# Softmax minus one-hot on one core: six row buffers used as pair, row, pair, row

## The chip, the cores and the metric

The kernel runs on 1 core of one Trainium2 chip. The time is that of the device, in microseconds, from one launch of the program; the median of the runs is compared. The profile is one execution of the same program, taken by the hardware profiler.

## The reference

The kernel computes the gradient of a cross entropy with respect to the logits: softmax along the last axis, minus one at the label. There are 8 x 1024 = 8192 vectors of 8192 float32, so 268.4 MB come in and 268.4 MB go out.

```python
batch, seq_len, vocab = 8, 1024, 8192
logits_max = np.max(logits, axis=-1, keepdims=True)
exp_logits = np.exp(logits - logits_max)
softmax = exp_logits / np.sum(exp_logits, axis=-1, keepdims=True)
one_hot[batch_idx, seq_idx, labels] = 1.0
return (softmax - one_hot).astype(np.float32)
```

## The kernel before, in words

The 8192 vectors are cut into B = 32 blocks of 256. In a block, partition p owns the two vectors 2p and 2p+1, which are neighbours in memory: 64 KB in one run. A "row" in this document is one vector for each of the 128 partitions, that is, one half j = 0 or 1 of a block: a tile of 128 x 8192 float32, 4 MB, with 32 KB in each partition. There are T = 64 rows, t = 2 x block + j. A row is loaded by one DMA, in 128 runs of 32 KB whose starts lie 64 KB apart in memory, and it is stored in the same way from the same buffer.

The tile X holds R = 6 row buffers (three slots of G = 2). Row t uses buffer t mod 6. Five instructions work on a row, and everything is done in place in its buffer:

- DVE `row_max`: a reduction to the negative maximum.
- ACT `row_exp`: exp(x - max), with the sum beside it.
- DVE `invert`: the reciprocal of the sum, 128 numbers.
- ACT `row_scale`: the exponentials times that reciprocal.
- DVE `subtract`: minus one where the iota equals the label.

Three engines carry their own order, and semaphores tie them together. SP issues all 64 loads in the order of the rows; from row 6 on, a load waits until the store of the row that had the buffer before has landed (semaphore `put`, one for each buffer; `got` tells that a load has landed). DVE runs, for each row, `invert(k)`, `row_max(k+1)`, `subtract(k)`. ACT runs `row_scale(k)`, `row_exp(k+1)`, and then issues `store(k)`, which waits for `subtract(k)`. Loads therefore go through SP's DMA queue (q1 in the profile) and stores through ACT's (q10). Both queues are served by the same 16 DMA engines. Every load and every store is spread over all 16: each engine moves 8 runs and then writes 4 bytes, its part of the count on the semaphore.

DVE and ACT have loops over ten rounds of six rows, and four rows follow written out. The last row is scaled and subtracted in quarters and stored in two halves of 2 MB. At the end ACT waits for all stores.

Every instruction of the loops is recorded at the helper `run`, so in the profile they all stand under L67, and the tiles' names tell them apart: `m<-X` is `row_max`, `X<-X,m` is `row_exp`, `X<-X,r` is `row_scale`, `X<-iota,lab,X` is `subtract`, `X<-in_logits_dram` is a load and `out_dram<-X` a store.

Of the kernel before, what the change touches and what calls it, by code (L numbers as in the profile page):

```python
# [6 lines left out]

P = 128
G = 2
SLOTS = 3  # L10
R = SLOTS * G


LAST = 4


@with_exitstack
def kernel(
# [23 lines left out]
    psum = ctx.enter_context(tc.tile_pool(name="psum", bufs=1, space=bass.MemoryType.PSUM))  # L42


    X = const.tile([P, SLOTS, G, V], fp32)
    lab_raw = const.tile([B, G * P], labels.dtype)
    lab_f = const.tile([B, G, P], fp32)
    ident = const.tile([B, B], fp32)
    lab = const.tile([P, G, B], fp32)
# [5 lines left out]

    with tc.tile_critical():  # L56
        sem = tc.alloc_semaphore
        got = [[sem(f"got{i}{q}") for q in range(2)] for i in range(SLOTS)]
        put = [[sem(f"put{i}{q}") for q in range(2)] for i in range(SLOTS)]
        lab_got, dve, pe, pool = (sem(n) for n in ("lab_got", "dve", "pe", "pool"))  # L60
        count = {}

        def run(engine, waits, counter, method, **operands):

            for w in waits[:-1]:
                engine.wait_ge(*w)
            instruction = getattr(engine, method)(**operands)  # L67
# [15 lines left out]

        made = X[:, SLOTS - 1, G - 1, :].bitcast(i16)[:, :V]
# [23 lines left out]
        def slot(k):  # L108
            return X[:, k // G, k % G, :]

        def column(a, k):
            return a[:, k : k + 1]

        def load(t):
            b, j = divmod(t, G)
            k = t % R
            after = [(put[k // G][q], t // R * 16) for q in range(G)] if t >= R else []
            after = after[j : j + 1] or [w_iota] * (t == R - 1)
            run(nc.sync, after, got[k // G][j], "dma_start", out=slot(k), in_=x_b[b, :, j, :])

        def row_max(k, n):
            run(
                nc.vector, [(got[k // G][k % G], n)], max_of[k % G], "tensor_reduce",
                out=column(m, k), in_=slot(k), axis=mybir.AxisListType.X, op=Alu.max, negate=True,
            )

        def row_exp(k, n):
            run(
                nc.scalar, [(max_of[k % G], n)], exp_of[k % G], "activation", out=slot(k),
                in_=slot(k), func=Act.Exp, bias=column(m, k), scale=1.0, accum_out=column(s, k),  # L130
            )

        def invert(k, n):
            run(
                nc.vector, [(exp_of[k % G], n)], inv_of[k % G], "reciprocal",
                out=column(r, k), in_=column(s, k),
            )

        def row_scale(k, n, c=slice(0, V)):
            run(  # L140
                nc.scalar, [(inv_of[k % G], n)], scl_of[k % G], "activation", out=slot(k)[:, c],
                in_=slot(k)[:, c], func=Act.Copy, bias=0.0, scale=column(r, k),
            )

        def subtract(k, n, label, c=slice(0, V)):
            run(
                nc.vector, [(scl_of[k % G], n)], sub_of[k % G], "scalar_tensor_tensor",
                out=slot(k)[:, c], in0=iota[:, c], scalar=label, in1=slot(k)[:, c],
                op0=Alu.is_equal, op1=Alu.subtract, reverse1=True,
            )  # L150

        def store(k, n, target, c=slice(0, V)):
            run(
                nc.scalar, [(sub_of[k % G], n)], put[k // G][k % G], "dma_start",
                out=target[:, c], in_=slot(k)[:, c],
            )
# [6 lines left out]
        ROUNDS = T // R  # L163
        for t in range(T):
            load(t)

        row_max(0, 16)
        row_exp(0, 1)

        done = [counter(nc.vector, q + 1) for q in range(SLOTS)]  # L170
        landed = counter(nc.vector, 16)
        with nc.vector.Fori(0, ROUNDS * SLOTS, SLOTS) as b:  # L172
            for k in range(R):
                invert(k, done[k // G])
                if k == R - 1:
                    nc.vector.reg_add(landed, landed, 16)
                row_max((k + 1) % R, landed)
                subtract(k, done[k // G], lab[:, k % G, bass.ds(b + k // G, 1)])
            for reg in done:
                nc.vector.reg_add(reg, reg, SLOTS)  # L180

        done = [counter(nc.scalar, q + 1) for q in range(SLOTS)]
        with nc.scalar.Fori(0, ROUNDS * SLOTS, SLOTS) as b:
            for k in range(R):
                row_scale(k, done[k // G])
                if k == R - 1:
                    for reg in done[: SLOTS - 1]:
                        nc.scalar.reg_add(reg, reg, SLOTS)
                row_exp((k + 1) % R, done[(k + 1) % R // G])
                target = o_b[bass.ds(b + k // G, 1), :, k % G, :]  # L190
                store(k, done[k // G], target.rearrange("o p v -> (o p) v"))
            nc.scalar.reg_add(done[-1], done[-1], SLOTS)

        for t in range(ROUNDS * R, T - 1):
            k, n = t % R, t // G + 1
            invert(k, n)
            row_max(k + 1, 16 * (ROUNDS + 1))
            row_scale(k, n)
            row_exp(k + 1, n + k % G)
            subtract(k, n, lab[:, t % G, t // G : t // G + 1])  # L200
            store(k, n, o_b[t // G, :, t % G, :])
        k, n = (T - 1) % R, B
        invert(k, n)
        for q in range(4):
            c = slice(q * V // 4, (q + 1) * V // 4)
            row_scale(k, n, c)
            subtract(k, n + q, lab[:, G - 1, B - 1 : B], c)
        half = V // 2
        store(k, n + 1, o_b[B - 1, :, G - 1, :], slice(0, half))
        store(k, n + 3, o_b[B - 1, :, G - 1, :], slice(half, V))  # L210
        stored = {}
        for t in range(T):
            stored[t % R] = stored.get(t % R, 0) + 16
        stored[k] += 16
        for q in sorted(range(R), key=lambda q: (q - k - 1) % R):
            nc.scalar.wait_ge(put[q // G][q % G], stored[q])


# [28 lines left out]
```

## Time and profile before

| what | value |
|---|---|
| median of 3 runs | 1247.61 us (1247.56 to 1247.7) |
| the profiled execution's own time: its span, first to last instruction | 1245.6 us |
| DVE busy | 1121.8 us, 90% |
| ACT busy | 919.4 us, 74% |
| bytes moved by DMA | 536.95 MB, mean 431 GB/s |
| DMA packets on the load queue, on the store queue | 9216, 9408 |

No other time of the profiled execution is known than its span; the median of the runs is 2.0 us longer, and that difference is taken as what lies around the span. A share of DMA is the mean over the 16 engines of the time that their packets took; 1.00 means that all 16 always had a packet in work. A packet is counted where it starts, so in a window of few packets the shares and rates are coarse.

### The profile page before, as it was taken

To read this page: it belongs to the slowest core of one execution; us is meant where nothing else is said; L and a number is where in the kernel's file an instruction comes from. 1 tells how busy PE (TensorE), PEld (TensorE's weight loads), DVE (VectorE), ACT (ScalarE), POOL (GpSimd) and SP (SyncE) were. 2 spreads that over 40 slices of the span, in tenths; PEclk is the share of its full clock that TensorE was granted. 3 is DMA by queue.
4 is the path that set the end of the run, shared out by engine and by line. 5 is a ranking of instruction groups with operands and counts; after the bars stand their busy time and mean duration, and the time that the engine had idled before them with its cause. 6 is when DMAs were issued, how large, how long until landed. Compare 5 with 4: busy or idle time off the path is not lost.

```text
span 1245.6 us, 868 instructions
## 1 busy us (share of the span) xinstructions
PE 0.4 (0%) x2; PEld 0.3 (0%) x2; DVE 1121.8 (90%) x198; ACT 919.4 (74%) x196; POOL 7.4 (1%) x7
## 2 busy tenths in 40 slices
PE   0000000000000000000000000000000000000000
PEld 0000000000000000000000000000000000000000
DVE  5999999999988989889898898988988989889893
ACT  3888888888767777777767777677777777777772
POOL 2000000000000000000000000000000000000000
DMA  9999999999999999999999999999999999999999
GB/s 406 418 426 436 438 434 425 438 438 429 429 438 436 427 434 438 435 426 436 438 432 426 438 438 428 430 438 435 428 434 438 434 427 436 437 434 426 438 436 389
DMA packets 18625, 536.95 MB, mean 431 GB/s; under 512 B 2080, under 2 KB 2080, under 8 KB 2112
## 3 DMA queue, kind: packets, MB, share of 16 engines
q1 hardware_dynamic: 9216, 268.44, 50.0%
q10 hardware_dynamic: 9408, 268.51, 49.9%
q14 instruction: 1, 0.01, 0.0%
HBM read 268.50 MB, written 268.44 MB: 431 GB/s over the span
## 4 chain that ended last, share of the span: by engine, by line
another core or an unknown queue 67%; DVE 21%; DMA 6%; issue 2%; SPq 1%; DVEq 0%; ACT 0%; ACTq 0%; PE 0%
DVE m L67 11%; DVE X L67 10%; DMA out_dram<-X 4%; DMA X<-in_logits_dram 2%; SPq L67 1%; DVE iota L67 0%; DVE lab_f L67 0%; DMA lab_raw<-in_labels_dram 0%; DVEq L56 0%; ACT X L67 0%; DVE r L67 0%; PE iota L67 0%; ACTq L67 0%; DVEq L172 0%
## 5 line engine op out<-in xcount | busy, mean ns | idle before, releaser
L67 DVE TENSOR_REDUCE m<-X 128x1 f32<-128x8192 f32 x64 | 555.6, 8681 | 90.6 <-DMA X<-in_logits_dram 90.6
L67 ACT ACTIVATE X<-X,m 128x8192 f32<-128x8192 f32 x64 | 455.8, 7122 | 184.8 <-DVE m L67 184.8
L67 DVE SCALAR_TENSOR_TENSOR X<-iota,lab,X 128x8192 f32<-128x8192 int16 (+1 forms) x67 | 559.8, 8360 | 2.4 <-ACT X L67 2.4
L67 ACT ACTIVATE X<-X,r 128x8192 f32<-128x8192 f32 (+1 forms) x67 | 456.4, 6816 | 118.2 <-DVE r L67 118.2
L67 DVE RECIPROCAL r<-s 128x1 f32<-128x1 f32 x64 | 9.8, 153 | 7.3 <-ACT X L67 7.3
L67 ACT ACTIVATION_READ_ACCUMULATOR X<-X,m 128x1 f32 x64 | 11.9, 186 | 0.0
L67 DVE CAST lab_f<-lab_raw 32x256 f32<-32x256 int32 x1 | 3.8, 3784 | 4.6 <-DMA lab_raw<-in_labels_dram 4.6
L67 POOL IOTA X<- 128x8192 int16 x1 | 6.9, 6943 | 0.0
L67 DVE TENSOR_SCALAR iota<-X 128x4096 int32<-128x4096 int32 x1 | 4.4, 4428 | 0.1
L67 ACT ACT_TABLE_LOAD x1 | 1.3, 1283 | 1.4 <-SPq L56 1.4
L67 DVE COPY lab<-iota 128x64 f32<-128x64 f32 x1 | 0.2, 225 | 0.5 <-PE iota L67 0.5
L67 PE MATMUL iota<-ident,lab_f 32*128 32x32 f32 x2 | 0.4, 298 | 8.5 <-DVE lab_f L67 8.5
L67 PEld LDWEIGHTS iota<-ident,lab_f 32*128 32x128 f32 x2 | 0.3, 192 | 8.4 <-DVE lab_f L67 8.4
L67 POOL TENSOR_SCALAR_AFFINE_SELECT ident<-ident 32x32 f32<-32x32 f32 x1 | 0.2, 202 | 0.1
L67 POOL MEMSET ident<- 32x32 f32 x1 | 0.1, 114 | 0.5 <-SPq L56 0.5
L231 POOL MEMSET const-bfloat16-1.0<- 128x1 bf16 x1 | 0.1, 107 | 0.0
L231 POOL MEMSET const-uint8-127<- 128x1 uint8 x1 | 0.1, 107 | 0.0
L231 POOL MEMSET const-float32-0.0<- 128x1 f32 x1 | 0.1, 104 | 0.2 <-issue 0.2
L231 POOL MEMSET const-float32-1.0<- 128x1 f32 x1 | 0.1, 104 | 0.0
## 6 DMA issues: line engine op xcount, KB each, us to landing
X<-in_logits_dram SPq DMA_DIRECT2D x64, 4096.0 KB, 24.2
out_dram<-X ACTq DMA_DIRECT2D x63, 4096.0 KB, 55.2
out_dram<-X ACTq DMA_DIRECT2D x2, 2048.0 KB, 16.9
lab_raw<-in_labels_dram ACTq DMA_DIRECT2D x1, 64.0 KB, 3.7
```

The lines of the kernel that those rows point to most:

```text
L67: instruction = getattr(engine, method)(**operands)
L231: nc = _bacc.Bacc("TRN2", target_bir_lowering=False, num_devices=1)
```

## The change: what it does

The six buffers are seen as four units: a pair (buffers 0 and 1), a row (2), a pair (3 and 4), a row (5). In a cycle of six rows (three blocks, c = 0 to 9), the table `PLACES` gives each buffer its half-block: the first pair is both halves of the cycle's block 0, buffer 2 has half 0 of block 2, the second pair is block 1, and buffer 5 has half 1 of block 2. The third block is thus still moved in two separate rows, with another pair between them. After ten cycles four rows remain (`LAST_PLACES`).

A pair can be moved whole: one DMA of 8 MB with 128 runs of 64 KB. `whole_load` does so for 17 of the 20 pairs (all but the first three), `whole_store` for 18 of the 20 (all but the first and the last). So there are 47 load DMAs in place of 64, and 47 store DMAs (the two halves of the last row among them) in place of 65. The pairs at both ends and the last four rows are moved by row as before.

A whole store is issued once, after `subtract` of the pair's second row; a whole load waits for the store that empties both of its buffers, and `row_max` of a pair's second row needs no wait of its own. The instructions on DVE and ACT, their shapes and their order by row stay the same. Since the ends differ from the middle, the first two cycles on DVE and the first and the last on ACT are written out, and the loops cover the others.

```diff
+R = 6
+PLACES = ((0, 0), (0, 1), (2, 0), (1, 0), (1, 1), (2, 1))
+LAST_PLACES = ((0, 0), (0, 1), (1, 0), (1, 1))
+PAIRS = (0, 3)
...
+        def whole_load(c, k):
+            return c < CYCLES and k in PAIRS and c * len(PAIRS) + PAIRS.index(k) >= 3
+
+        def whole_store(c, k):
+            return k in PAIRS and 1 <= c * len(PAIRS) + PAIRS.index(k) < CYCLES * len(PAIRS) - 1
...
+        def pair(k):
+            return X[:, k : k + G, :].rearrange("p j v -> p (j v)")
...
+        def load(c, k, n):
+            after = [free_at[c - 1, i] for i in range(k, k + n)] if c else []
+            after = after[:1] if len(set(map(str, after))) == 1 else after
+            after = after or [w_iota] * (k == R - 1)
+            b, j = places(c)[k]
+            block = x_b[c * BLOCKS + b]
+            if n > 1:
+                run(
+                    nc.sync, after, got[k], "dma_start",
+                    out=pair(k), in_=block.rearrange("p j v -> p (j v)"),
+                )
+            else:
+                run(nc.sync, after, got[k], "dma_start", out=row(k), in_=block[:, j, :])
...
+        def store_pair(k, n, target):
+            run(
+                nc.scalar, [(sub_of[(k + G - 1) % G], n)], put[k], "dma_start",
+                out=target.rearrange("p j v -> p (j v)"), in_=pair(k),
+            )
...
+            for k in range(R):
+                b, j = PLACES[k]
                 row_scale(k, done[k // G])
...
                 row_exp((k + 1) % R, done[(k + 1) % R // G])
+                target = o_b[bass.ds(first + b, 1), :, :, :].rearrange("o p j v -> (o p) j v")
+                if k - 1 in PAIRS:
+                    store_pair(k - 1, done[k // G], target)
+                elif k not in PAIRS:
+                    store(k, done[k // G], target[:, j, :])
```

More of the change, by code (lines that the diff above doesn't have):

```diff
@@ L9 @@
 G = 2
-SLOTS = 3
-R = SLOTS * G
-LAST = 4
+R = 6
+PLACES = ((0, 0), (0, 1), (2, 0), (1, 0), (1, 1), (2, 1))
+LAST_PLACES = ((0, 0), (0, 1), (1, 0), (1, 1))
+PAIRS = (0, 3)
 @with_exitstack
@@ L57 @@
         sem = tc.alloc_semaphore
-        got = [[sem(f"got{i}{q}") for q in range(2)] for i in range(SLOTS)]
-        put = [[sem(f"put{i}{q}") for q in range(2)] for i in range(SLOTS)]
+        got = [sem(f"got{k}") for k in range(R)]
+        put = [sem(f"put{k}") for k in range(R)]
         lab_got, dve, pe, pool = (sem(n) for n in ("lab_got", "dve", "pe", "pool"))
@@ L111, in column, with row @@
+        def row(k):
+            return X[:, k, :]
+        def pair(k):
+            return X[:, k : k + G, :].rearrange("p j v -> p (j v)")
         def column(a, k):
             return a[:, k : k + 1]
[L114 to L119, printed above, removed]
@@ L121, in row_max @@
-        def row_max(k, n):
-            run(
-                nc.vector, [(got[k // G][k % G], n)], max_of[k % G], "tensor_reduce",
-                out=column(m, k), in_=slot(k), axis=mybir.AxisListType.X, op=Alu.max, negate=True,
+        units = [
+            (c, k, G if k in PAIRS and k + 1 < len(places(c)) else 1)
+            for c in range(CYCLES + 1)
+            for k in range(len(places(c)))
+            if k - 1 not in PAIRS
+        ]
+        landed, stored = [0] * R, [0] * R
+        loaded_by, free_at = {}, {}
@@ new lines @@
+        for c, k, n in units:
+            for q in [k] if whole_load(c, k) else range(k, k + n):
+                landed[q] += 16
+                for i in range(k, k + n) if whole_load(c, k) else [q]:
+                    loaded_by[c, i] = (got[q], landed[q])
+            for q in [k] if whole_store(c, k) else range(k, k + n):
+                stored[q] += 16 + 16 * ((c, k) == units[-1][:2] and q == k + n - 1)
+                for i in range(k, k + n) if whole_store(c, k) else [q]:
+                    free_at[c, i] = (put[q], stored[q])
@@ L125, in row_max @@
+        for c, k, n in units:
+            if whole_load(c, k):
+                load(c, k, n)
+            else:
+                for q in range(k, k + n):
+                    load(c, q, 1)
+        def row_max(k, waits):
+            run(
+                nc.vector, waits, max_of[k % G], "tensor_reduce",
+                out=column(m, k), in_=row(k), axis=mybir.AxisListType.X, op=Alu.max, negate=True,
             )
@@ L147, in subtract @@
                 nc.vector, [(scl_of[k % G], n)], sub_of[k % G], "scalar_tensor_tensor",
-                out=slot(k)[:, c], in0=iota[:, c], scalar=label, in1=slot(k)[:, c],
+                out=row(k)[:, c], in0=iota[:, c], scalar=label, in1=row(k)[:, c],
                 op0=Alu.is_equal, op1=Alu.subtract, reverse1=True,
@@ L153, in store @@
             run(
-                nc.scalar, [(sub_of[k % G], n)], put[k // G][k % G], "dma_start",
-                out=target[:, c], in_=slot(k)[:, c],
+                nc.scalar, [(sub_of[k % G], n)], put[k], "dma_start",
+                out=target[:, c], in_=row(k)[:, c],
+            )
[3 more added lines that the diff above has]
+                out=target.rearrange("p j v -> p (j v)"), in_=pair(k),
             )
@@ L161, in counter, with nth, following @@
             return reg
[L163 to L172, printed above, removed]
-            for k in range(R):
+        def nth(c, k):
+            return c * BLOCKS + k // G + 1
+        def following(c, k):
+            return (c, k + 1) if k + 1 < len(places(c)) else (c + 1, 0)
@@ new lines, in vector_row, with scalar_row @@
+        def vector_row(c, k):
+            b, j = places(c)[k]
+            invert(k, nth(c, k))
+            row_max(following(c, k)[1], [loaded_by[following(c, k)]])
+            subtract(k, nth(c, k), lab[:, j, c * BLOCKS + b : c * BLOCKS + b + 1])
+        def scalar_row(c, k):
+            b, j = places(c)[k]
+            block = o_b[c * BLOCKS + b]
+            row_scale(k, nth(c, k))
+            row_exp(following(c, k)[1], nth(*following(c, k)))
+            if whole_store(c, k):
+                return
+            if k - 1 in PAIRS and whole_store(c, k - 1):
+                store_pair(k - 1, nth(c, k), block)
+            else:
+                store(k, nth(c, k), block[:, j, :])
@@ new lines @@
+        run_of = [c for c in range(CYCLES) if all(whole_load(c, k) for k in PAIRS)]
+        store_run = [c for c in range(CYCLES) if all(whole_store(c, k) for k in PAIRS)]
+        row_max(0, [loaded_by[0, 0]])
+        for c in range(run_of[0]):
+            for k in range(R):
+                vector_row(c, k)
+        c = run_of[0]
+        done = [counter(nc.vector, nth(c, G * q)) for q in range(BLOCKS)]
+        arrived = counter(nc.vector, loaded_by[c, 0][1])
+        with nc.vector.Fori(c * BLOCKS, (run_of[-1] + 1) * BLOCKS, BLOCKS) as first:
+            for k in range(R):
+                b, j = PLACES[k]
@@ L174 @@
                 invert(k, done[k // G])
                 if k == R - 1:
-                    nc.vector.reg_add(landed, landed, 16)
-                row_max((k + 1) % R, landed)
-                subtract(k, done[k // G], lab[:, k % G, bass.ds(b + k // G, 1)])
+                    nc.vector.reg_add(arrived, arrived, 16)
+                q = (k + 1) % R
+                row_max(q, [] if q - 1 in PAIRS else [(got[q], arrived)])
+                subtract(k, done[k // G], lab[:, j, bass.ds(first + b, 1)])
@@ L179 @@
             for reg in done:
-                nc.vector.reg_add(reg, reg, SLOTS)
-        done = [counter(nc.scalar, q + 1) for q in range(SLOTS)]
-        with nc.scalar.Fori(0, ROUNDS * SLOTS, SLOTS) as b:
-            for k in range(R):
+                nc.vector.reg_add(reg, reg, BLOCKS)
+        last_rows = len(LAST_PLACES)
+        for k in range(last_rows - 1):
+            vector_row(CYCLES, k)
+        row_exp(0, 1)
+        for c in range(store_run[0]):
+            for k in range(R):
+                scalar_row(c, k)
@@ L185 @@
+        c = store_run[0]
+        done = [counter(nc.scalar, nth(c, G * q)) for q in range(BLOCKS)]
+        with nc.scalar.Fori(c * BLOCKS, (store_run[-1] + 1) * BLOCKS, BLOCKS) as first:
+            for k in range(R):
+                b, j = PLACES[k]
                 row_scale(k, done[k // G])
                 if k == R - 1:
-                    for reg in done[: SLOTS - 1]:
-                        nc.scalar.reg_add(reg, reg, SLOTS)
+                    for reg in done[: BLOCKS - 1]:
+                        nc.scalar.reg_add(reg, reg, BLOCKS)
@@ L189 @@
                 row_exp((k + 1) % R, done[(k + 1) % R // G])
[L190 to L201, printed above, removed]
@@ L202 @@
-        k, n = (T - 1) % R, B
+                target = o_b[bass.ds(first + b, 1), :, :, :].rearrange("o p j v -> (o p) j v")
[3 more added lines that the diff above has]
+                    store(k, done[k // G], target[:, j, :])
+            nc.scalar.reg_add(done[-1], done[-1], BLOCKS)
+        for c in range(store_run[-1] + 1, CYCLES):
+            for k in range(R):
+                scalar_row(c, k)
@@ L203 @@
+        for k in range(last_rows - 1):
+            scalar_row(CYCLES, k)
+        k = last_rows - 1
+        b, j = LAST_PLACES[k]
+        n = nth(CYCLES, k)
+        b += CYCLES * BLOCKS
         invert(k, n)
@@ L206 @@
             row_scale(k, n, c)
-            subtract(k, n + q, lab[:, G - 1, B - 1 : B], c)
+            subtract(k, n + q, lab[:, j, b : b + 1], c)
         half = V // 2
[L209 to L214, printed above, removed]
+        store(k, n + 1, o_b[b, :, j, :], slice(0, half))
+        store(k, n + 3, o_b[b, :, j, :], slice(half, V))
         for q in sorted(range(R), key=lambda q: (q - k - 1) % R):
-            nc.scalar.wait_ge(put[q // G][q % G], stored[q])
+            nc.scalar.wait_ge(put[q], stored[q])
 _INS = ['logits', 'labels']
```

18 lines of the change are left out of this document (10 added, 8 removed).

## The prediction

> **What bounds the kernel now.** I read the page first, its DMA lines before its engines.
>
> ```profile
> span 1245.6 us, 868 instructions
> PE 0.4 (0%) x2; PEld 0.3 (0%) x2; DVE 1121.8 (90%) x198; ACT 919.4 (74%) x196; POOL 7.4 (1%) x7
> DMA  9999999999999999999999999999999999999999
> DMA packets 18625, 536.95 MB, mean 431 GB/s; under 512 B 2080, under 2 KB 2080, under 8 KB 2112
> q1 hardware_dynamic: 9216, 268.44, 50.0%
> q10 hardware_dynamic: 9408, 268.51, 49.9%
> X<-in_logits_dram SPq DMA_DIRECT2D x64, 4096.0 KB, 24.2
> out_dram<-X ACTq DMA_DIRECT2D x63, 4096.0 KB, 55.2
> out_dram<-X ACTq DMA_DIRECT2D x2, 2048.0 KB, 16.9
> ```
>
> The packets of the two queues fill 99.9% of the 16 engines' time, so the DMA engines set the time. 9216 packets for 64 loads are 144 a load: 128 runs of 32 KB and 16 small ones, so each engine takes 8 runs and then writes 4 bytes. A load lands 24.2 us after its issue, a store only 55.2 us after: stores queue up, and that queue is the cushion that keeps the engines fed. Next the windows, columns: start:end, length, busy time of each engine, clock, DMA share, GB/s.
>
> ```profile
> 52.20:61.88 9.68, 0.00 (x0) 0.00 (x0) 9.68 (x2) 8.58 (x2) 0.00 (x0) 1.00 1.00 433
> 100.00:1190.00 1090.00, 0.00 (x0) 0.00 (x0) 1001.37 (x173) 825.93 (x173) 0.00 (x0) 1.00 1.00 433
> ```
>
> A row moved one way costs 4.194 MB / 433 GB/s = 9.69 us of all engines, and from 100 to 1190 us no DMA time is lost. DVE is next. The chain of waits shows its pace while data are plentiful, and then the pace once they are not (the engine named there is unknown, the steps are those of SP's loads):
>
> ```profile
> 133.57 8.59 DVE m L67
> 142.15 7.35 DVE X L67
> 149.50 1.22 issue
> 150.88 8.58 DVE m L67
> ...
> 322.04 18.97 another core or an unknown queue
> ...
> 1155.04 19.01 another core or an unknown queue
> ```
>
> DVE needs 150.88 - 133.57 = 17.31 us a row; from 322.04 to 1155.04 there are 43 rows, 19.37 us each, two moves of 9.69. So the change can gain only by making the moves cheaper, and loses whatever leaves both queues empty at once. A wait on an engine counts only through that.
>
> **Part 1: what longer runs save.** Three windows of the DMA view give the price of one packet: 16 of 32 KB (75.15 to 76.4), 64 of 16 KB (1240 to 1242.4), and 16 of 4 bytes (the q1 line of 71.3 to 75.15). Columns: packets, MB, share of 16 engines.
>
> ```profile
> q1 hardware_dynamic: 16, 0.52, 97.0%
> q10 hardware_dynamic: 64, 1.05, 101.8%
> q1 hardware_dynamic: 16, 0.00, 0.2%
> ```
>
> 32 KB take 0.970 x 1.25 = 1.2125 us, 16 KB 1.018 x 2.4 x 16 / 64 = 0.6108 us, 4 bytes 0.002 x 3.85 = 8 ns. So 2 x 0.6108 - 1.2125 = 9 ns of a packet do not depend on its length. Neighbours overlap a little: 19.37 us hold 16 packets and two small ones, so one costs (19.372 - 0.016) / 16 = 1.2098 us net, 6 ns above 2 x (1.2125 - 0.6108) = 1.2034 for its bytes: of the 9 ns about 6 count. A pair moved whole has 8 runs an engine in place of 16 and one count in place of two: 8 x 6 + 8 = 56 ns. There are 17 whole loads and 18 whole stores: 35 x 56 ns = 2.0 us. Ends: 2.8 us if the full 9 ns count, 0.3 us if a run of 64 KB goes as two packets and only the counts go. No row has a run above 32 KB; from 16 to 32 KB the price per byte only falls, so I take 2.0.
>
> The Trainium skill ("DMA: Bandwidth & Descriptors", Anatomy of one DMA) prices a DMA at about 2.0 us fixed plus its bytes at 436 GB/s. By it 35 DMAs fewer would be worth 70 us, an estimate from that page. The trace disagrees: moves follow each other at 9.68 us with a share of 1.00, so that latency lies under other moves.
>
> **Part 2: what the order costs.** Arithmetic and its order on DVE and ACT are the same; ACT issues 18 stores less, SP 17 loads less, which is free: neither bounds. What moves is when a buffer comes free. The first row of a pair waits one DVE row (17.3 us) for the second before it is stored, and that comes out of the stores' cushion. A load pair behind it waits on SP, and the next single load is queued behind that.
>
> I carried both queues forward packet by packet, with five rules: a run costs 1.21 us (32 KB) or 2.41 us (64 KB); queues that both hold work alternate by packet; DVE needs 17.3 us a row; a DMA begins 1.3 us after its issue when the engines stand; one that joins while the other queue runs begins 4.0 us after. The last two, from SP's and ACT's issues in the timeline and from the DMA view of 2.16 to 2.97 (none of q1 is earlier), of 73.3 to 75.15 and of 75.15 to 76.4:
>
> ```profile
> 0.96 13.06 SPq L67 DMA_DIRECT2D X<-in_logits_dram  x6
> 46.97 0.39 ACTq L67 DMA_DIRECT2D out_dram<-X  x1
> 71.22 18.47 SPq L67 DMA_DIRECT2D X<-in_logits_dram  x2
> ...
> q1 hardware_dynamic: 16, 0.52, 188.5%
> ...
> q10 hardware_dynamic: 16, 0.52, 65.6%
> ```
>
> The first load, issued at 0.96, begins on all 16 engines within 1.2 to 2.0 us. The load issued at 71.22 has no packet before 75.15 (its 16 first ones are the 97.0% line above); the stores had the engines alone for a turn. From a landing to the instruction that waits for it I put 0.4 us, an estimate: the count takes less than one turn of 1.21.
>
> *The middle.* A cycle of three rows has 3 x 19.37 = 58 us of DMA and 3 x 17.3 = 51.9 us of DVE from the landing of a pair to the issue of its store (`row_max` and `subtract` three times). In the replay a pair lands at 398.7, its store is issued at 451.1, and the store of the row before has landed at 449.5: the store queue is dry for 8.5 us until 457.9, while the pair load (to 456.7) and then the single load run. The load queue is dry for about 4.5 us a cycle, while stores run. Never both: the middle costs nothing, 18 dry gaps included.
>
> *The start.* Row 0's store is issued at 46.97 and each next one 17.31 us later, so those of rows 3 and 4 at 98.9 and 116.2; as a pair both go at 116.2. Six loads, three stores and three loads before it are 12 x 9.69 = 116 us from 2.2 on, to 118.4, and the store can begin at 117.5: covered, by 1 us. If that fails, 0.5 us.
>
> *The end.* Before:
>
> ```profile
> 1178.95 8.69 DVE L67 TENSOR_REDUCE m<-X 128x1 f32<-128x8192 f32 x1 [1.96 <-DMA X<-in_logits_dram]
> 1198.31 8.69 DVE L67 TENSOR_REDUCE m<-X 128x1 f32<-128x8192 f32 x1 [1.94 <-DMA X<-in_logits_dram]
> 1206.91 8.74 DVE L67 SCALAR_TENSOR_TENSOR X<-iota,lab,X 128x8192 f32<-128x8192 int16 x1
> 1215.68 0.34 ACTq L67 DMA_DIRECT2D out_dram<-X  x1
> 1222.74 4.86 ACTq L67 DMA_DIRECT2D out_dram<-X  x2
> ```
>
> Row 63, the last, lands just before 1198.3. Row 62's store is issued 17.4 us later, after `row_max` of 63 and `subtract` of 62, and can begin 1.3 us after that. The stores queued at the landing must last 0.4 + 17.4 + 1.3 = 19.1 us, or the engines stand still. Before, they last: the halves land about 16.9 us after 1222.7 and 1227.3, so at 1244.3; less 19.4 for rows 62 and 63, there is work until 1224.9, 26.6 us.
>
> Changed: when the last pair store (rows 54, 55) lands, loads 60 to 63 and the stores of 56 to 63 remain. Load 60 begins 0.4 + 4.0 us later, and four whole packets of store 56 go alone. Then 32 load packets alternate with 31 of the stores. At the last landing 4 + 31 = 35 store packets are out: rows 56 to 59 and three packets of row 60. Five of row 60 and eight of row 61 are left: 13 x 1.21 = 15.7 us against 19.1. The engines stand for 3.4 us. If the loads return within 2 us, the cover is 18.1 and the loss about 0.9; a turn later, 4.6. I take 3.4, by the row at 71.22. After a standstill a first packet was slower: 1.885 x 0.81 = 1.53 us in the quoted row, against 1.21. I add 0.3.
>
> Sum against the profiled execution: 1245.6 - 2.0 + 3.4 + 0.3 = 1247.3; the median lies 2.0 above the span, so **1249.3**, 0.14% slower. Within 0.2% (2.5 us) is what I call the same, about what a measurement of this kernel can tell.
>
> **The rivals.**
>
> *Slower: each return of the stores stalls the engines.* Stores enter a stretch of loads alone only once in this trace, at the first store (issued at 46.97):
>
> ```profile
> 47.59:48.80 1.21, 0.00 (x0) 0.00 (x0) 1.21 (x1) 1.21 (x1) 0.00 (x0) 1.00 1.01 433
> 48.80:50.90 2.10, 0.00 (x0) 0.00 (x0) 2.10 (x1) 2.10 (x1) 0.00 (x0) 1.00 1.01 250
> 50.90:52.20 1.30, 0.00 (x0) 0.00 (x0) 1.30 (x1) 1.30 (x1) 0.00 (x0) 1.00 1.00 403
> ```
>
> From 48.8 a turn of load packets takes 2.10 us in place of 1.21, the next 1.30: 0.98 us lost on all 16 engines (share 1.01 says busy, 250 GB/s says stalled). If that is the price of every return after a dry gap, the 18 gaps cost 17.6 us: 1266.9. For it: the only such entry shows it. Against: it may be the first store's alone, and the load queue's return at 71.22 cost nothing. It decides at once: on top of the forecast's 1.7 us a single stall passes 2.5 us, and the kernel is slower.
>
> *Faster: the end stays covered.* If loads return early and the full 9 ns count, 1247.6 - 2.8 = 1244.8. For it: cover and need differ by 3.4 us only. Against: both must hold.
>
> *No longer runs.* If 64 KB go as two packets, only 0.3 us is saved: 1249.3 + 1.7 = 1251.0. The packet counts tell: 47 x 144 = 6768 on the load queue if whole, 64 x 128 + 47 x 16 = 8944 if cut.
>
> A page speaks against the change: the Trainium skill (the same page, Queues, rings and completion order) has each engine switch queues at packet boundaries, so a 64 KB packet beside a 32 KB one takes two thirds of the engine. The DMA view of 600 to 800 us agrees on alternation:
>
> ```profile
> q1 hardware_dynamic: 1488, 43.52, 50.4%
> q10 hardware_dynamic: 1472, 42.99, 49.8%
> ```
>
> Equal packets, equal bytes; with unequal runs the shares follow the runs, and that is in the second rule.
>
> **How the numbers follow.** Forecast 0.66, stalls at each return 0.24, cut runs 0.06, covered end 0.04. The forecast's own range is 1245.7 (saving 2.8, end 0.9, nothing else) to 1251 (end 4.6, saving 2.0, start 0.5 and the tenths); a quarter of it, 0.17, lies above 1250.1. Same: 0.49. Slower: 0.24 + 0.06 + 0.17 = 0.47. Faster: 0.04. The range must reach into the stalls: 1245.7 to 1267.
>
> **What would show it.** Right: 6768 packets on q1; a share of 1.00 in the middle, with dry gaps of about 8 us in q10 every 58 us; row 62's store issued about 17.4 us after the last landing, with a hole of some 3 us before it. Wrong: windows at the returns of the stores at 250 GB/s; 8944 packets; no hole near the end; a middle whose rate differs from 433 by more than 2.

## The result and the profile after

The changed kernel took **1305.23 us**, the median of five runs (1289.07 to 1306.9), beside 1247.61 for the kernel before: a ratio of 1.0434 [1.0385, 1.0482], slower by 57.6 us. The forecast was 1249.3. (A ratio is that of the means over the executions within 1.5% of the fastest of their kernel, so it can lie off the quotient of the medians.) The trace belongs to the fastest of the five executions (span 1287.3); the other four took 1301.57 to 1306.9 and have no trace, so the readings below account for 41.7 of the 57.6 us.

From the page of the kernel after: the span, the engines, the DMA lines, the costliest wait of DVE, and the DMA issues with their median time from issue to landing.

```profile
span 1287.3 us, 749 instructions
PE 0.4 (0%) x2; PEld 0.3 (0%) x2; DVE 1116.3 (87%) x198; ACT 919.3 (71%) x196; POOL 7.4 (1%) x7
...
DMA packets 13586, 536.96 MB, mean 417 GB/s; under 512 B 1520, under 2 KB 1520, under 8 KB 1552
...
q1 hardware_dynamic: 6768, 268.44, 49.7%
q10 hardware_dynamic: 6816, 268.50, 48.8%
...
L66 DVE TENSOR_REDUCE m<-X 128x1 f32<-128x8192 f32 x64 | 555.1, 8673 | 142.7 <-DMA X<-in_logits_dram 142.7
...
X<-in_logits_dram SPq DMA_DIRECT2D x30, 4096.0 KB, 37.5
out_dram<-X ACTq DMA_DIRECT2D x27, 4096.0 KB, 32.7
...
out_dram<-X ACTq DMA_DIRECT2D x18, 34.6
X<-in_logits_dram SPq DMA_DIRECT2D x17, 33.3
```

The engines' arithmetic is what it was (ACT 919.3 us busy against 919.4, DVE 1116.3 against 1121.8). The load queue has the 6768 packets of whole 64 KB runs. Packets fill 49.7 + 48.8 = 98.5% of the span, 1268.0 us of each DMA engine, where they filled 99.9% of 1245.6, 1244.4 us: with fewer packets and the same bytes they took 23.6 us more. The engines stood idle for 19.3 us instead of 1.2, which is 18.1 more. The two sums make up the 41.7; since the page rounds the shares, each is good to about 2 us. The stores' cushion went from 55.2 us to about 33.

Where it went, by windows (columns as in the prediction):

```profile
100.00:1190.00 1090.00, 0.00 (x0) 0.00 (x0) 953.44 (x166) 793.54 (x166) 0.00 (x0) 1.00 0.99 421
646.40:652.86 6.46, 0.00 (x0) 0.00 (x0) 4.25 (x3) 4.63 (x3) 0.00 (x0) 1.00 0.96 304
1211.40:1287.30 75.90, 0.00 (x0) 0.00 (x0) 58.62 (x13) 46.33 (x13) 0.00 (x0) 1.00 0.84 360
1261.90:1265.80 3.90, 0.00 (x0) 0.00 (x0) 3.20 (x2) 2.07 (x3) 0.00 (x0) 1.00 0.00 0
```

The last stretch of the same length in the kernel before:

```profile
1169.70:1245.60 75.90, 0.00 (x0) 0.00 (x0) 51.24 (x12) 42.16 (x12) 0.00 (x0) 1.00 0.96 415
```

The middle lost 1090 x (1 - 421/433) = 30 us, about evenly over its length (422, 420 and 420 GB/s from 100 to 400, to 800 and to 1190); the end lost 75.9 x (415 - 360)/433 = 9.6 us. The second row shows one spot in close-up: 304 GB/s at a share of 0.96, so most of the loss there is packets that take longer, not engines without work. It ends at the first packet of a pair store.

What changed in kind is seen in the counts. Each of the 16 engines ends its part of a DMA with 4 bytes. In the kernel before all 16 counts of one store lie within 0.6 us (DMA view, 417.60 to 418.20; packets, MB, share):

```profile
q10 hardware_dynamic: 16, 0.00, 1.5%
```

After, the first ten counts of a pair store come between 272.55 and 272.95, and the last two only between 289.6 and 289.9 (the store queue's row of the first window, the packet row of the second):

```profile
q10 hardware_dynamic: 10, 0.00, 1.4%
...
DMA packets 8, 0.39 MB, mean 1311 GB/s; under 512 B 2, under 2 KB 2, under 8 KB 2
```

The 16 engines no longer run in step. Below, **spread** is the time from the first to the last of the 16 counts of one DMA, and **stall** is the time by which packets exceed their undisturbed duration (1.213 us for 32 KB, 2.418 us for 64 KB), per engine. Both are taken from the records of single counts and packets, over all DMAs of a trace. Before: mean spread 0.6 us, at most 1.0, stall 1.5 us in all. After: mean spread 5.4 us (loads) and 6.4 us (stores), at most 21.2; stall 26 us, 24 of it between 100 and 1190 us. There the engines stood idle for 7 us besides.

The stalls are not mainly in the long packets: 16.8 of the 26 us are in packets of 32 KB, and 10.8 of these in load packets that began while no store packet was in flight, that is, in the dry gaps of the store queue.

A DMA has landed when the last of its 16 counts has come, so its slowest engine decides. How that reaches the end is shown by the chain of waits (start, us, what):

```profile
286.22 36.36 DMA out_dram<-X
322.60 33.29 DMA X<-in_logits_dram
...
407.91 34.28 DMA out_dram<-X
442.22 35.52 DMA X<-in_logits_dram
...
477.76 0.07 DVE m L66
...
529.76 32.16 DMA out_dram<-X
```

A pair's buffers go round in a closed loop: pair store, pair load into the same buffers, three rows of DVE (52.0 us, from 477.76 to 529.76), pair store. From 407.91 to 529.76 that is 34.28 + 35.52 + 52.0 = 121.8 us for six rows, where the DMA engines need 6 x 19.37 = 116.2. In this stretch of the chain nothing waits for anything outside the loop.

### The profile page after: what moved, and what is told of

The parts are those of the page before. It is cut to its first block, busy times and chain, and to the rows that moved or that the text cites. A ratio compares the mean times of both kernels' runs of the same rounds, so it can differ in the third digit from the quotient of the medians.

```text
span 1287.3 us, 749 instructions
## 1 busy us (share of the span) xinstructions
PE 0.4 (0%) x2; PEld 0.3 (0%) x2; DVE 1116.3 (87%) x198; ACT 919.3 (71%) x196; POOL 7.4 (1%) x7
## 3 DMA queue, kind: packets, MB, share of 16 engines
q1 hardware_dynamic: 6768, 268.44, 49.7%
q10 hardware_dynamic: 6816, 268.50, 48.8%
## 4 chain that ended last, share of the span: by engine, by line
DMA 49%; DVE 42%; issue 7%; ACT 1%; DVEq 0%; PE 0%; ACTq 0%; SPq 0%
DMA X<-in_logits_dram 25%; DMA out_dram<-X 24%; DVE X L66 22%; DVE m L66 19%; ACT X L66 1%; DMA lab_raw<-in_labels_dram 0%; DVE iota L66 0%; DVE r L66 0%; DVEq L55 0%; DVE lab_f L66 0%; DVEq L249 0%; PE iota L66 0%; DVEq L259 0%; ACTq L66 0%; DVE lab L66 0%
## 5 line engine op out<-in xcount | busy, mean ns | idle before, releaser
L66 DVE CAST lab_f<-lab_raw 32x256 f32<-32x256 int32 x1 | 1.1, 1077 | 7.3 <-DMA lab_raw<-in_labels_dram 7.3
```

## The experiments

The prediction's rival was that each return of the store queue after a dry gap stalls the engines (theory S where the expectations use a letter). Against it stood that long runs are themselves what costs, and that the new order or the held-back pair stores do. Most kernels come from one form of the changed kernel, with all cycles written out and two switches: whether a pair's load and its store move "whole" (one DMA, 64 KB runs), as "two" (issued where the whole one would be, after the same wait, but as two DMAs of 32 KB runs), or by "row" as in the kernel before. "Whole" in both places was not run in this form; where it is compared, the time is that of the changed kernel itself, which has loops. (`order_by_row` below says what writing out costs.)

**The order alone.**

```diff
-LOAD, STORE = "whole", "whole"
+LOAD, STORE = "row", "row"
```

> The changed kernel's order of half-blocks and buffers, but every load and store by row, 32 KB runs, each with its own wait; the loops are written out. Theory S (returns of a dry store queue stall the engines): no dry gaps, so as before, 1247.6 +- 1. Theory U (packets of 64 KB beside 32 KB drive the 16 engines apart): the same, 1247.6. A third cause, that the order of the half-blocks or the written-out code costs something: clearly above 1250.

Measured: 1248.19 us (1248.03 to 1248.67), ratio 1.0003 [0.9994, 1.0013]. The order of the half-blocks and the written-out loops cost nothing that can be told, all moves being by row.

**The waits without the long runs.**

```diff
-LOAD, STORE = "whole", "whole"
+LOAD, STORE = "two", "two"
```

> The changed kernel's order and waits: a pair is stored only after its second row and loaded only when both buffers are free, but as two DMAs of 4 MB, issued one behind the other, with runs of 32 KB. Theory S: the dry gaps remain, so most of the loss remains, 1285 to 1307. Theory U: no unequal packets, so the loss is gone; by the replay of the prediction, without stalls, 1249 to 1251.

Measured: nine executions from 1251.86 to 1274.57 us, median 1267.81, ratio 1.0110 [1.0073, 1.0147]. In the traced one, which is among the longer (1270.82), the mean spread of the loads was 9.7 us and the stall 14.0 us. Both expectations missed: holding pairs back costs 4 to 27 us without any long run, but not 57.

**Only the loads whole** (`loads_whole`).

```diff
-LOAD, STORE = "whole", "whole"
+LOAD, STORE = "whole", "row"
```

> Only the 17 pair loads are whole (64 KB runs, waiting for both buffers); every store goes by row as soon as its row is ready. Theory S: the load queue goes dry, the store queue hardly; a loss below half of the full one, 1248 to 1270. Theory U: unequal packets in one queue half of the time; about half of the loss, 1265 to 1285.

Measured: 1249.25 us, ratio 1.0011 [1.0002, 1.0021]. Spread 1.2 us for loads and 2.9 for stores, stall 2.0 us. Its chain of waits:

```profile
342.37 31.53 DMA out_dram<-X
373.91 33.58 DMA X<-in_logits_dram
407.52 8.69 DVE m L69
...
450.83 8.67 DVE X L69
459.52 30.58 DMA out_dram<-X
```

Its stores, with their median time to landing:

```profile
out_dram<-X ACTq DMA_DIRECT2D x63, 4096.0 KB, 31.0
```

The same closed loop, begun by the store of the pair's second row, takes 459.52 - 342.37 = 117.2 us this time; the middle runs at 433 GB/s, so 116.2 on average. So a loop without slack costs next to nothing while the spread is this small. Theory U, which had 1265 to 1285, missed; 1249.25 is in the range of theory S.

**Only the stores whole** (`stores_whole`).

```diff
-LOAD, STORE = "whole", "whole"
+LOAD, STORE = "row", "whole"
```

> Only the 18 pair stores are whole (64 KB runs, after the second row); loads go by row in 32 KB runs. Theory S: the store queue still runs dry each cycle, so most of the loss, 1280 to 1307. Theory U: about half of the loss, as in loads_whole, 1265 to 1285.

Measured: 1274.34 us (1269.62 to 1285.48), ratio 1.0225 [1.0165, 1.0286]. Mean spread 14.1 us (loads) and 8.6 (stores), stall 16.5 us, idle 14.9. That is in the range of theory U, below that of theory S.

**The stores held back, but in 32 KB runs.** The stores have short runs. But one thing more differs from the last kernel than the expectation below says: a row's load waits here for the store of its own row alone, where in the last kernel it waits for the whole pair's store. So loads go out earlier.

```diff
-LOAD, STORE = "whole", "whole"
+LOAD, STORE = "row", "two"
```

> Stores held as in the changed kernel, two DMAs of 32 KB runs issued one behind the other after the pair's second row; loads by row. Beside stores_whole (1274) it differs in the run length of the stores alone. Theory S: dry gaps as in stores_whole, so 1265 to 1280. Theory L: run length decides, so 1249 to 1256.

Measured: 1251.55 us (1250.66 to 1252.5), ratio 1.0031 [1.0016, 1.0045], spread 2.0 and 2.3 us. Whole stores, with the later loads that they bring, cost 1274.34 - 1251.55 = 22.8 us here. The windows of 100 to 1190, stores whole:

```profile
100.00:1190.00 1090.00, 0.00 (x0) 0.00 (x0) 968.09 (x167) 800.30 (x167) 0.00 (x0) 1.00 1.00 426
```

and as two:

```profile
100.00:1190.00 1090.00, 0.00 (x0) 0.00 (x0) 995.85 (x172) 823.04 (x172) 0.00 (x0) 1.00 1.00 432
```

Both have a share of 1.00; only the rate tells that packets stall. The issues of stores, with their median time to landing, first whole, then as two:

```profile
out_dram<-X ACTq DMA_DIRECT2D x27, 4096.0 KB, 34.5
...
out_dram<-X ACTq DMA_DIRECT2D x18, 32.3
...
out_dram<-X ACTq DMA_DIRECT2D x63, 4096.0 KB, 50.9
```

As two, the stores keep most of the cushion of 55.2 us, and their queue stood empty for more than 2 us only twice after the first 20 us, against 19 times when whole. Theory S had assumed the same dry gaps, so this pair of runs does not part the length of a run from the dry gaps. The next one does.

**Loads whole, stores as two.**

```diff
-LOAD, STORE = "whole", "whole"
+LOAD, STORE = "whole", "two"
```

> The changed kernel with its whole loads, but each pair's stores as two DMAs of 32 KB runs issued together after the second row. Beside the changed kernel (1305) it differs in the run length of the stores alone. If long runs in the store queue cause the loss (they take two thirds of an engine beside a 32 KB load and empty the store queue sooner): 1250 to 1270. If joint loads beside held stores cause it whatever the run: 1285 to 1307.

Measured: 1262.03 us, ratio 1.0116 [1.0095, 1.0137]. Here the waits are those of the changed kernel, and so is the cushion:

```profile
out_dram<-X ACTq DMA_DIRECT2D x63, 4096.0 KB, 32.3
```

The store queue runs dry as it does there (31 gaps over 2 us, 145 us in all, against 36 and 138). So the stores' run length alone (and with it the number of DMAs) is worth 1305.23 - 1262.03 = 43 us (24 to 47 between single executions). The switches together, median us:

| loads \ stores | row | two of 32 KB | whole |
|---|---|---|---|
| row | 1248.2 | 1251.6 | 1274.3 |
| two of 32 KB | | 1267.8 | |
| whole | 1249.3 | 1262.0 | 1305.2 |

The effects don't add up: whole loads cost 1 us beside stores by row, 10 beside stores held back, 31 beside whole stores. Where loads and stores wait as in the changed kernel, whole loads take no longer than loads as two (1262.0 beside 1267.8), and only the stores' run length costs (43 us). The joint waits, with whole loads, are worth the step from 1248.2 to 1262.0, about 14 us.

**Removing the dry gaps.** `row_max` reduces a quarter of the columns, so DVE is faster and stores come earlier; once with pairs whole, once by row.

```diff
-                out=column(m, k), in_=row(k), axis=mybir.AxisListType.X, op=Alu.max, negate=True,
+                out=column(m, k), in_=row(k)[:, : V // 4], axis=mybir.AxisListType.X, op=Alu.max, negate=True,
```

> The changed kernel (pairs whole, 64 KB runs, stores held for the second row), written out, with row_max over a quarter of the columns only: three quarters of the maximum are left out, and DVE gets about 6 us a row faster. The DMAs, their order and their runs stay; by the replay the stores are then issued early enough that the store queue has no dry gap after the first 110 us. Theory S (returns of a dry store queue): nearly the whole loss goes, 1245 to 1251. Theory L (long or unequal runs, or the held pairs themselves, are what costs): still 1285 to 1307.

> Control for the run before: row_max over a quarter of the columns (the rest of the maximum is left out), everything by row in 32 KB runs. Both theories: DMA bound as before, 1247 to 1248.5.

Measured: whole 1277.91 us (1273.1 to 1300.07), with a stall of 25 us and mean spreads of 9.4 us (loads) and 14.0 (stores); by row 1255.12 (1248.26 to 1266.88), with hardly any stall but a spread of the loads of up to 6.6 us. With pairs whole the store queue was empty for more than 2 us only once after the first 20 us (5.4 us). The stalls stay without the long dry gaps, so S is not the whole cause; the time missed both ranges. The control was disturbed itself, which was not expected: the pair is weak evidence.

**Half of the pairs.**

```diff
-FIRST_LOAD, LAST_LOAD = 3, 20
-FIRST_STORE, LAST_STORE = 1, 19
+FIRST_LOAD, LAST_LOAD = 3, 11
+FIRST_STORE, LAST_STORE = 1, 10
```

> The changed kernel with only half of its pairs whole (8 loads, 9 stores, in the first half of the program), the rest by row. A fixed price for each return: half of the loss, about 1275. A disturbance that feeds itself (engines drift apart further from gap to gap): less than half, 1255 to 1270.

Measured: 1267.84, 1269.41, 1291.89 and 1292.11 us, ratio 1.0167 (the lower two). In the trace, that of 1267.84, the spread rose to 11.5 us in the first half and was back at 1.4 once moves went by row, so the engines fall into step again by themselves. The lower two lost 21 us, less than half of the loss, the other two 44: four executions don't tell a fixed price from a disturbance that feeds itself.

**DMAs alone.** To see whether the queues do this without any compute, the next kernels have no arithmetic: 128 row loads into four buffers in turn, and stores of two buffers that are loaded once. What a store waits for sets how the store queue is fed. First all stores queued at the start (`dma_backlog`), then one after every two loads (`dma_returns`).

```diff
             if PER == 1:
                 b, j = divmod(i, G)
-                waits = [landed[1]]
+                waits = [landed[2 * i + 1]]
                 w = run(nc.scalar, waits, put, "dma_start", out=o_b[b, :, j, :], in_=X[:, 4 + j, :])
```

> DMAs alone, all arithmetic left out: 128 row loads of 4 MB into four buffers in turn (the queue always backlogged), and 64 row stores from two other buffers, all issued at the start. 194 moves of 9.69 us: 1880 us, with one entry of the store queue. It is the zero of the next run.

> The same moves, arithmetic left out, but each store is issued when two more loads have landed, so the store queue is dry for about 9 us before each of 64 stores, beside a load queue that never is. Theory S (each return stalls the 16 engines by 0.9 to 1.0 us): 57 to 63 us above dma_backlog. Rival (the stall belongs to the first store alone): within 3 us of it.

Measured: 1887.85 and 1889.3 us. In the second the store queue is dry for about 10 us before each store after the first, and next to nothing stalls after the first store: the 64 returns cost 1.5 us together, not the 57 to 63 of theory S. From its DMA view:

```profile
DMA packets 27937, 813.72 MB, mean 431 GB/s; under 512 B 3104, under 2 KB 3104, under 8 KB 3104
...
q1 hardware_dynamic: 18720, 545.27, 67.0%
q10 hardware_dynamic: 9216, 268.44, 32.9%
```

**Returns with pair stores,** 32 of 64 KB runs, one per four loads (`dma_returns_64k`).

```diff
-        PER = 1
+        PER = 2
-            waits = [landed[2 * i + 1]]
+            waits = [landed[2 * i + 3]]
```

> As dma_returns, arithmetic left out, but two rows are stored at once in 64 KB runs after each four loads: 32 returns. Theory S with the same price: 29 to 32 us above dma_backlog, less 2 us for the longer runs. If a return of long runs costs more: above 40. Rival (first store alone): within 3 us of dma_backlog.

Measured: 1946.52 us (1939.35 to 1953.69), 57 more than dma_returns. In the trace, that of 1939.35, mean spread of the loads 17.8 us, stall 46.6 us (24.5 in the long packets), idle 8.8. Its DMA view, the GB/s in 40 slices of the span first:

```profile
GB/s 411 422 434 433 431 430 433 431 432 430 409 423 422 435 415 419 418 416 423 416 417 416 419 431 417 418 424 419 421 420 420 421 420 419 433 421 423 405 421 329
DMA packets 23329, 813.71 MB, mean 420 GB/s; under 512 B 2592, under 2 KB 2592, under 8 KB 2592
...
q1 hardware_dynamic: 18720, 545.27, 66.3%
q10 hardware_dynamic: 4608, 268.44, 33.2%
```

Shares nearly as before, bytes as before, 50 us more span: the packets themselves take longer, with no compute and no loop to wait for. And it doesn't come with each return: slices 3 to 10 run at 430 to 434 GB/s, most later ones at 415 to 424.

**The length of the gap.** Longer gaps at 32 KB (a store per three loads, 192 loads; `gap_20us_32k`), and shorter ones at 64 KB (a pair store per two loads, 64 loads; `gap_9us_64k`).

```diff
-        LOADS = 2 * T
+        LOADS = 3 * T
-            waits = [landed[2 * i + 1]]
+            waits = [landed[3 * i + 2]]
```

```diff
-        LOADS = 2 * T
+        LOADS = 1 * T
-        PER = 1
+        PER = 2
-            waits = [landed[2 * i + 1]]
+            waits = [landed[i + 1]]
```

> As dma_returns (arithmetic left out, 32 KB runs), but a store after every third load: 258 moves and dry gaps of about 20 us in place of 11. At the 9.71 us a move of dma_backlog 2509 us without any stall. Theory G (the price of a return rises with the length of the gap, whatever the run): 20 to 55 us more. If short runs never pay: within 4 us of 2509.

> As dma_returns_64k (arithmetic left out, 64 KB store runs), but a pair store after every second load, so the gaps are about 9 us in place of 25: 130 moves, 1265 us without stalls (9.71 us a move, 4 us around). Theory G: within 6 us of that. Theory M: 32 pair stores cost as in dma_returns_64k, 40 to 65 us more.

Measured: 2511.05 us, and its bytes at 431 GB/s (1082.16 MB) make 2511; 1330.57 us, where 545.27 MB at 431 make 1265. In the traces the gaps are 19.7 and 6.8 us on average. At 32 KB the length of the gap costs nothing, and the long runs cost 65 us over 32 pair stores with gaps a quarter as long as in dma_returns_64k (25.7 us). Two 32 KB stores issued together, the same burst in short runs, were not run without compute; the kernel with loads whole and stores as two is the nearest.

**Long runs without gaps.** 64 KB stores all queued at the start beside 32 KB loads (below; `dma_backlog_64k`), then both queues with 64 KB (the loads as in the next diff).

```diff
-        PER = 1
+        PER = 2
-            waits = [landed[2 * i + 1]]
+            waits = [landed[1]]
```

> As dma_backlog (DMAs alone, all arithmetic left out, 1887.85 us), but the 64 rows are stored as 32 pairs in 64 KB runs, all issued at the start: long store runs beside short load runs, no return. If only returns are dear (theory R): 1886, the 2 us of part 1 gained. If a long store run stalls beside short load runs wherever they meet (theory M): 1920 to 1960.

> As dma_backlog_64k (arithmetic left out), with the loads as pairs in 64 KB runs as well: equal runs in both queues. Theory M in the form that unequal runs are dear: back to 1884 to 1887. In the form that long store runs are dear by themselves: as dma_backlog_64k.

Measured: 1887.76 us in one execution and 1916.63 in the other; both long, 1887.37 (1886.58 to 1888.17). The trace of the first is that of 1887.76 us, its spread at most 1.0 us. Long runs beside short ones are free there, with the engines in step; what happened in the execution of 1916.63 us is not known, since it has no trace. The first one's DMA view from 200 to 600 us:

```profile
q10 hardware_dynamic: 1985, 115.41, 66.6%
q1 hardware_dynamic: 1984, 57.67, 33.4%
```

**Returns with long runs on the other side, or on both.**

```diff
-        for t in range(LOADS):
+        for t in range(0, LOADS, G):
...
-            landed.append(run(nc.sync, after, got[k], "dma_start", out=X[:, k, :], in_=x_b[b, :, j, :]))
+            w = run(
+                nc.sync, after, got[k], "dma_start", out=X[:, k : k + G, :].rearrange("p j v -> p (j v)"),
+                in_=x_b[t % T // G].rearrange("p j v -> p (j v)"),
+            )
+            landed += [w, w]
```

> As dma_returns_64k (arithmetic left out, 32 pair stores of 64 KB runs, each after four rows have landed; 1939 to 1954 us), with the loads as pairs in 64 KB runs too. If unequal runs are the condition: 1884 to 1892. If a long store run on a return is dear by itself: 1935 to 1955.

> The inequality turned round, arithmetic left out: loads as pairs in 64 KB runs, 64 row stores in 32 KB runs, one after each two rows landed (as dma_returns, 1889.3 us). With both runs long the time was 1908, between the two theories. If any inequality of runs is dear on returns: 1920 to 1960. If only the long store is: 1884 to 1892, as loads_whole (1249.25 beside 1247.77) suggests.

Measured: 1908.27 us with both long (+19 over dma_returns), 1921.3 with only the loads long (+32). The mean spread of the loads was 15.5 and 16.7 us. So long runs in either queue can do it, and long stores beside short loads are the dearest. But in the last kernel the store queue did not run dry: each store was issued 1 to 15 us before the one before it had landed. So a queue that runs dry is no condition of the loss.

## Why the prediction was wrong

**Part 1 was right for a packet, but its 2.0 us never showed as time.** Runs go whole (6768 packets). An undisturbed 64 KB packet takes 2.418 us, two of 32 KB take 2 x 1.213: 8 ns saved, against 9 forecast, of which 6 were to count. But with both queues backlogged, 96 DMAs fewer, with nearly all bytes in 64 KB runs, took 1887.37 us against 1887.85: 0.5 us, where 96 x 56 ns would be 5.4. And whole loads took 1249.25 us where rows took 1248.19. The price of about 2.0 us a DMA, which part 1 quotes from the Trainium skill ("DMA: Bandwidth & Descriptors", Anatomy of one DMA), is fitted there to DMAs issued from GpSimd, and these are issued from SP and ACT; the 0.5 us for 96 DMAs agrees with part 1 that such a latency lies under other moves. The median packet of the changed kernel has just these durations; the loss lies in a tail, which lifts the mean of its 32 KB load packets from 1.216 us before to 1.279.

**The start was nearly right:** 427 GB/s from 2 to 100 us against 429 is 0.5 us, where the forecast had none and named 0.5 in case the cover failed.

**The end was right in place and size, not in sum.** Row 62's store is issued 17.4 us after the last landing, as forecast, and the hole, 3.9 us of it in the window above, was forecast with 3.4. But the last 75.9 us lost 9.6 us, where 3.7 were forecast. The rest is engines without work around the hole, not stalls, which are 0.4 us there: the counts of the last load lie 8.4 us apart, those of the store before the hole 5.8.

```profile
1247.68 8.69 DVE L66 TENSOR_REDUCE m<-X 128x1 f32<-128x8192 f32 x1 [2.26 <-DMA X<-in_logits_dram]
...
1265.06 0.34 ACTq L66 DMA_DIRECT2D out_dram<-X  x1
```

**The step that failed is "Never both: the middle costs nothing, 18 dry gaps included".** It cost 30 us in the traced execution, and the middle ran at 421 GB/s, well beyond the 2 off 433 that the prediction named as a sign of being wrong. The overlap itself came close: the engines stood idle for 7 us of the middle. What failed is the price of a packet: the replay gave each queue one course, as if the 16 engines were one, and every packet its undisturbed duration, and packets took 24 us more. For six rows the DMA engines need 116.2 us, and DVE takes 52.0 of a pair's loop, which leaves 64.2 us for its store and its load; the trace has 34.28 + 35.52 = 69.8. The smaller cushion does not explain it alone, nor does the loop without slack: with only the loads whole the cushion is 31.0 us, and such a loop runs at 433 GB/s (1249.3). What the runs show in place of the failed step: with the waits unchanged the stores' 64 KB runs cost 43 us, the joint waits cost about 14, and stores of 64 KB bring stalls with no loop of compute at all (+57 in the DMAs alone).

**The rival named the place and had the wrong mechanism.** Its price, 0.98 us from the first store, was that store's alone: 64 returns of 32 KB stores cost 1.5 us together. The larger part goes with the length of the stores' runs (43 us), the smaller with the joint waits (about 14). Nor is it a price per return: 57/32 = 1.8 and 65/32 = 2.0 us per pair store in the DMA-only kernels are means, and the slices 3 to 10 above show returns of 64 KB stores that cost nothing.

**Alternation by packet held.** The Trainium skill ("DMA: Bandwidth & Descriptors", Queues, rings and completion order) has an engine switch queues at packet boundaries; the DMA view of 200 to 600 us above has 1985 packets beside 1984, and two thirds of the engines' time for the longer ones. A turn is one run there: around 300 us the 16 engines begin a store's run (299.9), then a load's (302.3), a store's (303.5), a load's (305.9). So the replay's second rule stands where both queues hold work.

**Open.** What inside the DMA path makes a packet longer when engines are out of step wasn't found: the trace has only start and end of a packet. A spread is no loss by itself: with both queues long and never dry it stayed at 4.5 us and cost nothing. Nor is it known whether the spread makes packets longer or longer packets make the spread. Load packets alone are not slow as such: in dma_returns 9899 of them began with no store packet in flight and stalled 2.1 us in all, against 10.8 us for 1248 in the changed kernel. Why pairs held back at 32 KB drift in most executions, why a faster DVE by row does, and what the four executions without a trace lost beyond the 41.7 us, is open too. No version tried was faster than the kernel before.

## What to carry to other kernels

Where the DMA engines were full, a longer run saved next to nothing (8 ns on 2.4 us of a packet, no time that showed), and with the waits that came with it it cost 57 us. In these runs short runs with queues kept fed were the safe choice. A replay of queues that treats 16 engines as one can't show them drifting apart; ask how much slack each buffer's loop has for the slowest one. Look at the rate beside the DMA share and at how far the 16 counts of one DMA lie apart: a share of 1.00 at 426 GB/s is a loss that the share doesn't show.

## What was not expected of the hardware

- The 16 engines can fall out of step within a queue, in DMAs that give each the same bytes: by up to 21 us in the changed kernel, 41 us in dma_returns_64k and 62 us in gap_9us_64k. They can get back into step within the run (11.5 to 1.4 us with half of the pairs).
- In the changed kernel the 32 KB packets of the loads kept their median of 1.213 us while their mean rose to 1.279: one in twenty took over 1.83 us.
- One program runs at different speeds: 1887.76 and 1916.63 us for one kernel of DMAs alone, and within one execution of dma_returns_64k 430 to 434 GB/s in slices 3 to 10, mostly 415 to 424 after.
- In the kernels without drift the loads stalled once by about 1 us at the first store (1.1 us in the kernel before, 0.9 in dma_returns); the later returns of 32 KB stores in dma_returns did not stall them.
